# Experts' tokens by indirect DMA, and seven experts' results as DRAM rows, in a two-layer trunk on one core

## The chip, the core and the metric

The program runs on one NeuronCore of one Trainium2 chip. Its five engines run their own instruction streams in order and wait for each other through semaphores: TensorE (PE, matrix products and transposes into PSUM), VectorE (DVE), ScalarE (ACT), GpSimd (POOL) and SyncE (SP, which here only issues DMAs). ACT, POOL and SP can issue DMAs. The metric is the device time of one execution in microseconds (us); the number to be forecast is the median over several runs.

## The reference, cut to what matters

The model is a trunk of two layers over 256 latent tokens of width 1024. The second layer ends in a mixture of experts: each token picks two of eight experts, and each expert is a SwiGLU whose three matrices have 1024 x 3584 elements, all float32.

```
def moe_swiglu(h, w_router, b_router, w_gate, w_up, w_down):
    logits = (h @ w_router + b_router).astype(jnp.float32)
    top_v, top_i = lax.top_k(logits, TOP_K)              # TOP_K = 2
    weights = jax.nn.softmax(top_v, axis=-1)
    combine = jnp.sum(jax.nn.one_hot(top_i, N_EXPERTS) * weights[..., None], axis=-2)
    y = jnp.zeros_like(h)
    for e in range(N_EXPERTS):                           # 8
        y = y + combine[..., e:e + 1] * swiglu(h, w_gate[e], w_up[e], w_down[e])
    return y
...
    h_lat = modulate(rms_norm(x, norm_g[layer, 1]), sh_f, sc_f)
    x = x + g_f[:, None, :] * ffn(h_lat)
    return rms_norm(x, final_g)
```

## The kernel before

The change lies in the expert stage, the last 1000 us of the program. Everything else streams weights through the same machinery and stays as it is.

**Weights.** They come in units of 1 MB (128 x 2048 float32). SP loads each unit into one of 11 buffers of a ring (`load`, L162). To get float32 accuracy, a unit is split into a high part `wh` (ACT, L177) and a low part `wl` (DVE, L178), each in 3 rotating buffers, and each product is three matmuls of 512 columns (`mm3`, L214 to L216): high times high, low times high, high times low. One unit feeds 12 matmuls.

**Experts.** An expert holds up to 128 tokens and takes seven chunks of its hidden width. A chunk is six units: two of the gate and two of the up matrix (`expert_in`, the result is `a`), four transposes of `a` (`turn`, L1043), and two of the down matrix (`expert_out`), whose sums over the chunks stay in two PSUM tiles `ys` until the expert ends. That is 72 matmuls a chunk and 56 chunks. A branch at the end repeats an expert for tokens beyond 128; it isn't taken for these inputs.

**Getting the tokens.** The normalized residual lies as tokens x features in two SBUF tiles, `hth` (high part) and `htl` (low part). `pos` gives each token's place in each expert. `slots` makes the 256 x 128 one-hot matrix `S` of an expert on DVE (L961), and `gather` multiplies it with `hth` and `htl` for each of 8 blocks of 128 features (L996, 32 matmuls of 128 columns; the first two experts take 48, since the row scale is not yet in the tiles). ACT (L1000) and DVE (L1001) add the shift and make the high and low part of `xg`, the experts' input. Expert 0's gather runs at once, before anything else of the stage; the others run in the background of the expert before. `normalize` scales `hth` and `htl` in the background after that.

**Adding the results.** When experts 0 to 6 end, `scatter_steps` takes `ys` times the gate `gf` (DVE, L1070), splits it into `yh` and `yl`, multiplies with the transposed one-hot matrix `ST` (`slots_T`, L1063, two transposes; L1077, eight matmuls of 512 columns), and DVE adds the result with the token's weight to the accumulator `acc` (L1079). Expert 7 does the same without the split (`scatter_now`), since nothing is left to hide it. In expert 7's fourth chunk two loads fetch `fg`, the final norm's gain, into the buffers that `yh` and `yl` had:

```
fg = [mop.tile([P, 512], F32, tag=t, name=nm("fg"), bufs=1) for t in ("yh", "yl")]
for n in range(2):
    nc.scalar.dma_start(fg[n], A["fg_row"][:, 512 * n:512 * n + 512])
```

**Order.** The code is written in Tile: a scheduler sets each engine's order and the semaphores from the code's order and its own estimate of times, so background work is placed where it sees room. Tiles of one tag share their buffers, and whoever takes a buffer waits for its last reader.

Of the kernel before, what the change touches and what calls it, by code (L numbers as in the profile page):

```python
# [8 lines left out]
F32 = mybir.dt.float32  # L9
# [7 lines left out]
P = 128  # L17
KD = 8
# [94 lines left out]
def _program(tc, A, out):  # L113
# [10 lines left out]
    smallp = tc.alloc_tile_pool(name="smallp", bufs=2)  # L124
    xp = newpool("xp", 1, "right")
    pools = [const, rawp, whp, psp, smallp, xp]
# [119 lines left out]
    mc = const.tile([P, 392], F32, tag="mc", name="mc")  # L246
# [733 lines left out]
    def gather(p_, e, raw=False):  # L980
        S = []
        xg = mop1.tile([P, KD, 2, P], F32R, tag="xg", name=nm("xg"), bufs=2)

        def steps():
            if raw:
                s_ = slots(p_, e, "yh", rsh.bitcast(F32))
                terms = [(hth, s_), (htl, s_), (hth, slots(p_, e, "yl", rsl))]
            else:
                S.append(slots(p_, e))
                terms = [(hth, S[0]), (htl, S[0])]  # L990
            yield
            for k in range(KD):
                pg = ps_mm() if front and k % 2 else ps_t()
                for i_, (hsrc, s_) in enumerate(terms):
                    for tt in range(2):
                        pe.matmul(pg[:, 0:P], lhsT=hsrc[:, tt, k * P:k * P + P], rhs=s_[:, tt * P:tt * P + P],  # L996
                                  start=(i_ == 0 and tt == 0), stop=(i_ == len(terms) - 1 and tt == 1))
                b = mod[:, 1, 24 + k, 0:1]
                hi, lo = xg[:, k, 0, :], xg[:, k, 1, :]
                ia = act.activation(hi, pg[:, 0:P], AF.Identity, bias=b)  # L1000
                iv = vec.scalar_tensor_tensor(lo, pg[:, 0:P], b, hi.bitcast(F32), ALU.add, ALU.subtract)  # L1001
                hold[:] = [ia, iv] if front else []
                yield
            if raw:
                S.append(slots(p_, e))
        return xg, S, steps()

    front = []
# [76 lines left out]
    def scatter_steps(e, ys, ST):  # L1085
# [246 lines left out]
```

## Time and profile before

| what | value |
|---|---|
| runs | 1862.95, 1863.76, 1865.36 us (median 1863.76) |
| the profiled execution | 1863.94 us, its span 1862.1 us (1.84 us lie outside the span) |
| granted TensorE clock | full in every slice of the span |
| expert stage in that span | about 845 to 1846 us, then 16 us of last scatter, final norm and output |
| PE busy over the span | 1818.9 us, 98% |
| DVE, ACT busy over the span | 1331.7 us (72%), 1040.2 us (56%) |

Busy time is the time in which an engine had an instruction in work. PE's ends are modelled, so the distance from one matmul's start to the next one's is a better measure of its pace than the durations. All times of the trace are of the one profiled execution, counted from the span's start.

### The profile page before, as it was taken

How to read it: one execution, taken by the hardware profiler on the slowest of the kernel's cores; microseconds unless marked ns; L12 is line 12 of the kernel's file. 1: busy time of each engine (PE TensorE's matmuls, PEld its weight loads, DVE VectorE, ACT ScalarE, POOL GpSimd, SP SyncE). 2: the span in 40 equal slices, each digit the busy share in tenths (PEclk: the TensorE clock that was granted, in tenths of full speed). 3: DMA queues.
4: the chain of work that ended last, by engine and by line, in shares of the span. 5: the costliest groups of instructions: out<-in, count | busy, mean ns of one | idle time of the engine just before them, and what ended most of it. 6: DMA issues, size and time to landing. Idle time of an engine off the chain costs nothing. (4 is left out here: it accounts for less than half of the span.)

```text
span 1862.1 us, 22324 instructions
## 1 busy us (share of the span) xinstructions
PE 1818.9 (98%) x8878; PEld 1437.5 (77%) x8878; DVE 1331.7 (72%) x1452; ACT 1040.2 (56%) x1082; POOL 0.2 (0%) x4
## 2 busy tenths in 40 slices
PE   6999999999999999999999999999999999999997
PEld 4775487888888877488888888888888888888885
DVE  5632755443344586658899889898888898988987
ACT  3323634222222354646677777677777777777774
POOL 0000000000000000000000000000000000000000
PEclk9999999999999999999999999999999999999999
DMA  9567333232223254367999999999999999999890
GB/s 361 187 237 269 111 117 125 99 139 91 90 91 102 99 150 156 136 226 293 351 334 367 346 355 371 329 362 364 338 346 361 353 355 350 353 359 352 324 420 35
DMA packets 68688, 475.05 MB, mean 255 GB/s; under 512 B 7520, under 2 KB 8160, under 8 KB 13024
## 3 DMA queue, kind: packets, MB, share of 16 engines
q1 hardware_dynamic: 66416, 469.27, 68.0%
q10 hardware_dynamic: 2160, 4.27, 0.7%
q8 instruction: 72, 1.18, 0.2%
q14 instruction: 40, 0.33, 0.1%
HBM read 470.36 MB, written 1.05 MB: 253 GB/s over the span
## 5 line engine op out<-in xcount | busy, mean ns | idle before, releaser
L178 DVE TENSOR_TENSOR wl<-raw,wh 128x2048 fp32r<-128x2048 f32 (+1 forms) x461 | 904.9, 1984 | 242.4 <-ACT wh L177 238.1
L177 ACT ACTIVATE wh<-raw 128x2048 fp32r<-128x2048 f32 (+1 forms) x461 | 763.7, 1670 | 352.0 <-PE mm L215 133.6
L214 PE MATMUL mm<-wh,xg 128*128 128x512 f32 x896 | 353.4, 394 | 0.0
L215 PE MATMUL mm<-wl,xg 128*128 128x512 f32 x896 | 352.3, 393 | 0.0
L216 PE MATMUL mm<-wh,xg 128*128 128x512 f32 x896 | 349.9, 390 | 0.0
L215 PEld LDWEIGHTS mm<-wl,xg 128*128 128x128 f32 x896 | 168.4, 188 | 35.1 <-DVE wl L178 1.9
L216 PEld LDWEIGHTS mm<-wh,xg 128*128 128x128 f32 x896 | 168.4, 188 | 34.2
L214 PEld LDWEIGHTS mm<-wh,xg 128*128 128x128 f32 x896 | 168.4, 188 | 33.6
L214 PE MATMUL mm<-hx,wh 128*128 128x512 f32 (+1 forms) x496 | 189.0, 389 | 3.0 <-ACT hx L378 3.0
L215 PE MATMUL mm<-hx,wh 128*128 128x512 f32 (+1 forms) x496 | 191.4, 386 | 0.1
L216 PE MATMUL mm<-hx,wl 128*128 128x512 f32 (+1 forms) x496 | 191.0, 385 | 0.0
L215 PE MATMUL pss<-wl,ahi 128*128 128x512 f32 x448 | 176.7, 395 | 1.3 <-DVE wl L178 1.3
L216 PE MATMUL pss<-wh,alo 128*128 128x512 f32 x448 | 174.5, 390 | 0.0
L214 PE MATMUL pss<-wh,ahi 128*128 128x512 f32 x448 | 168.2, 391 | 0.0
L214 PEld LDWEIGHTS mm<-hx,wh 128*128 128x128 f32 x496 | 93.3, 189 | 26.3 <-ACT hx L378 3.4
L215 PEld LDWEIGHTS mm<-hx,wh 128*128 128x128 f32 x496 | 93.6, 189 | 18.7 <-DVE hx L380 0.5
L216 PEld LDWEIGHTS mm<-hx,wl 128*128 128x128 f32 x496 | 93.6, 189 | 18.7
L215 PEld LDWEIGHTS pss<-wl,ahi 128*128 128x128 f32 x448 | 84.2, 188 | 20.3 <-DVE wl L178 3.9
L214 PEld LDWEIGHTS pss<-wh,ahi 128*128 128x128 f32 x448 | 84.1, 188 | 17.2
L216 PEld LDWEIGHTS pss<-wh,alo 128*128 128x128 f32 x448 | 84.2, 188 | 16.7
L387 DVE SCALAR_TENSOR_TENSOR x<-mm,mod,x 128x256 f32<-128x256 f32 x120 | 52.4, 479 | 50.5 <-PE mm L216 50.5
L214 PE MATMUL mm<-ah,wh 128*128 128x512 f32 x176 | 68.6, 390 | 0.2
(275 smaller groups left out, 1975.7 us busy)
## 6 DMA issues: line engine op xcount, KB each, us to landing
raw<-in_mg SPq DMA_DIRECT2D x112, 1024.0 KB, 7.0
raw<-in_mu SPq DMA_DIRECT2D x112, 1024.0 KB, 7.1
raw<-in_md SPq DMA_DIRECT2D x112, 1024.0 KB, 6.9
raw<-in_ada SPq DMA_DIRECT2D x48, 1024.0 KB, 5.6
raw<-in_na_in SPq DMA_DIRECT2D x10, 1024.0 KB, 5.6
raw<-in_fg SPq DMA_DIRECT2D x10, 1024.0 KB, 4.9
raw<-in_fu SPq DMA_DIRECT2D x10, 1024.0 KB, 4.9
raw<-in_fd SPq DMA_DIRECT2D x10, 1024.0 KB, 4.9
```

What stands on the lines that cost most here:

```text
L177: act.activation(h_, r_, AF.Copy)
L178: vec.tensor_tensor(l_, r_, h_.bitcast(F32), ALU.subtract)
L214: pe.matmul(ps, lhsT=lh, rhs=rh, start=start, stop=False)
L215: pe.matmul(ps, lhsT=lh, rhs=rl, start=False, stop=False)
L216: pe.matmul(ps, lhsT=ll, rhs=rh, start=False, stop=stop)
L387: vec.scalar_tensor_tensor(x[:, db, a:b], ps[:, a:b], mod[:, l, g0 + db, c:c + 1], x[:, db, a:b], ALU.mult, ALU.add)
```

## The change

Two DRAM tiles are added: `hrow`, the 256 normalized tokens as rows of 1024 float32, and `yrow`, 7 x 128 rows for the results of experts 0 to 6. `normalize` now starts at once in the background: eight transposes and two ACT copies make the shift as rows, eight DVE operations make the complete token rows, and four POOL DMAs write them to `hrow`. Expert 0 is gathered as before (`first_gather_steps`). For experts 1 to 7 two small matmuls turn `S` into the list of token numbers, DVE converts it to integers, POOL issues one indirect DMA that fetches 128 rows (512 KB) into `xt`, and eight transposes in two groups with two splits make `xg`. When experts 0 to 6 end, ACT copies the two PSUM tiles `ys` to SBUF and issues two DMAs to `yrow` (`keep_rows`). `row_numbers` works out, for each token, its up to two rows in `yrow` and their weights; `combine`, in the background of expert 7, fetches them by four indirect DMAs of 512 KB and adds them to `acc`. Expert 7's own tokens are still added by `scatter_now`. Lines after the first hunk shift (L178 is L181 after, L1001 is L1005, L1043 is L1067, L1144 is L1213).

```diff
+    hrow = dramp.tile([TL, 1024], F32, tag="hrow", name="hrow")
+    yrow = dramp.tile([(NE - 1) * P, 1024], F32, tag="yrow", name="yrow")
...
     def normalize():
+        shift = []
+        for n in range(2):
+            pt = ps_t()
+            for j in range(4):
+                pe.transpose(pt[:, j * P:j * P + P], mod[:, 1, 24 + 4 * n + j, 0:1].to_broadcast([P, P]), ident)
+            shift.append(mop.tile([P, 512], F32, tag=("yh", "yl")[n], name=nm("shift"), bufs=1))
+            act.activation(shift[n], pt, AF.Copy)
+            yield
         for tt in range(2):
             for n in range(2):
...
-                    vec.tensor_scalar(t, l.bitcast(F32), r, None, ALU.mult)
+                    vec.scalar_tensor_tensor(t, l.bitcast(F32), r, shift[n], ALU.mult, ALU.add)
                 vec.scalar_tensor_tensor(t, h.bitcast(F32), r, t, ALU.mult, ALU.add)
+                nc.gpsimd.dma_start(hrow[tt * P:tt * P + P, 512 * n:512 * n + 512], t)
                 yield
-                put_split(h, l, t)
...
+    def gather(p_, e):
+        xg, S = new_xg(), []
+        def steps():
+            S.append(slots(p_, e))
+            yield
+            pi = ps_t()
+            for tt in range(2):
+                pe.matmul(pi[:, 0:2], lhsT=S[0][:, tt * P:tt * P + P].bitcast(F32), rhs=tokn[:, tt, :],
+                          start=(tt == 0), stop=(tt == 1))
+            idx = mop1.tile([P, 1], I32, tag="idx", name=nm("idx"), bufs=2)
+            vec.tensor_copy(idx, pi[:, 0:1])
+            xt = mop1.tile([P, 1024], F32, tag="htl", name=nm("xt"))
+            nc.gpsimd.indirect_dma_start(xt[:, :], None, hrow[:, :], bass.IndirectOffsetOnAxis(ap=idx[:, 0:1], axis=0))
+            for _ in range(4):
+                yield
+            for h in range(2):
+                pg = ps_t()
+                for j in range(4):
+                    pe.transpose(pg[:, j * P:j * P + P], xt[:, (4 * h + j) * P:(4 * h + j) * P + P], ident)
+                hi, lo = xg[:, 4 * h:4 * h + 4, 0, :], xg[:, 4 * h:4 * h + 4, 1, :]
+                put_split(hi, lo, pg.rearrange("p (k s) -> p k s", s=P))
+                yield
...
+    def keep_rows(e, ys):
+        for n in range(2):
+            yv = mop.tile([P, 512], F32, tag=("yh", "yl")[n], name=nm("yv"), bufs=1)
+            act.activation(yv, ys[n], AF.Copy)
+            nc.scalar.dma_start(yrow[e * P:e * P + P, 512 * n:512 * n + 512], yv)
+    def row_numbers():
...
+    def combine():
+        for tt in range(2):
+            yy = mop1.tile([P, 2, 1024], F32, tag="hth", name=nm("yy"))
...
+            for i_ in range(2):
+                vec.tensor_copy(ri[i_], rows[i_][0][:, tt:tt + 1])
+                nc.gpsimd.indirect_dma_start(yy[:, i_, :], None, yrow[:, :],
+                                             bass.IndirectOffsetOnAxis(ap=ri[i_][:, 0:1], axis=0))
+            for _ in range(3):
+                yield
+            for n in range(2):
+                h_ = slice(512 * n, 512 * n + 512)
+                a, b = yy[:, 0, h_], yy[:, 1, h_]
+                vec.tensor_scalar(a, a, rows[0][1][:, tt:tt + 1], None, ALU.mult)
+                vec.scalar_tensor_tensor(a, b, rows[1][1][:, tt:tt + 1], a, ALU.mult, ALU.add)
+                yield
+                vec.tensor_tensor(a, a, gf[:, h_], ALU.mult)
+                vec.tensor_tensor(acc[:, tt, h_], acc[:, tt, h_], a, ALU.add)
+                yield
...
     def finish():
         expert_out(prev["e"], prev["c"], prev, prev["ys"])
         if prev["c"] == NCH - 1:
-            pend[:] = [scatter_steps(prev["e"], prev["ys"], prev["ST"])]
-            next(pend[0])
+            keep_rows(prev["e"], prev["ys"])
...
-                ST = slots_T(S[0])
                 if e < NE - 1:
-                    nxt = gather(pos, e + 1, e == 0)
+                    nxt = gather(pos, e + 1)
                     background.append(nxt[2])
-                if e == 0:
-                    background.append(normalize())
+                else:
+                    ST = slots_T(S[0])
+                    background.append(combine())
+                if e == 1:
+                    background.append(row_numbers())
```

The scheduler decides where these pieces land, so three places of its order are shown.

On PE, while expert 2 runs, its order before holds the first of expert 3's eight gather groups between two chunks (`S_8744` is expert 3's one-hot matrix, `xg_7775` expert 2's input):

```order
L216 MATMUL pss_8552<-wh_8666,alo_8634 128x512
L1063 MATMUL pst_8719<-c_ident,S_7795 128x128 x2
L214 MATMUL mm_8725<-wh_8685,xg_7775 128x512
...
L216 MATMUL mm_8725<-wh_8703,xg_7775 128x512
L996 MATMUL pst_8765<-S_8744,hth 128x128 x2
L996 MATMUL pst_8765<-S_8744,htl 128x128 x2
L1043 MATMUL pst_8774<-c_ident,a_8626 128x128 x4
L214 MATMUL mm_8783<-wh_8728,xg_7775 128x512
```

After, PE makes the list of token numbers (L1016) and, one chunk of 72 matmuls later, transposes the first half of the fetched rows (L1027); a second chunk later, the second half:

```order
L217 MATMUL mm_8496<-wh_8462,xg_7699 128x512
L1016 MATMUL pst_8659<-tokn,S_8638 128x2 x2
L218 MATMUL mm_8496<-wl_8463,xg_7699 128x512
...
L217 MATMUL mm_8619<-wh_8584,xg_7699 128x512
L1027 MATMUL pst_8788<-c_ident,xt_8664 128x128 x4
L218 MATMUL mm_8619<-wl_8585,xg_7699 128x512
...
L217 MATMUL mm_8751<-wh_8717,xg_7699 128x512
L1027 MATMUL pst_8825<-c_ident,xt_8664 128x128 x4
```

The 32 gather matmuls and the two transposes L1063 are gone from the stretch; the index matmuls and the first transposes stand 72 matmuls apart, and that distance is the same for experts 3 to 7 (167 for expert 1, 72 for expert 2).

On DVE, at the first gather, the order before goes from the one-hot matrix `S` straight to the eight low parts of `xg` (six of the rows stand here):

```order
L961 TENSOR_SCALAR S_6438<-mc,pos_6340 128x128 x2
L1001 SCALAR_TENSOR_TENSOR xg_6359<-pst_6366,mod,xg_6359 128x128
L1001 SCALAR_TENSOR_TENSOR xg_6359<-mm_6375,mod,xg_6359 128x128
L1001 SCALAR_TENSOR_TENSOR xg_6359<-pst_6384,mod,xg_6359 128x128
L1001 SCALAR_TENSOR_TENSOR xg_6359<-mm_6393,mod,xg_6359 128x128
L1001 SCALAR_TENSOR_TENSOR xg_6359<-pst_6402,mod,xg_6359 128x128
```

After, the small operations of `row_numbers` stand there:

```order
L964 TENSOR_SCALAR S_6832<-mc,pos_6344 128x128 x2
L1119 TENSOR_SCALAR nw_7988<-pos_6344 128x16
...
L1128 TENSOR_REDUCE nr_8014<-nv_7987 128x2
L1005 SCALAR_TENSOR_TENSOR xg_6363<-pst_6370,mod,xg_6363 128x128
L1129 TENSOR_TENSOR ne_7989<-nv_7987,nr_8014 128x16
...
L1128 TENSOR_REDUCE nr_8057<-nv_7987 128x2
L1005 SCALAR_TENSOR_TENSOR xg_6363<-mm_6379,mod,xg_6363 128x128
L1129 TENSOR_TENSOR ne_7989<-nv_7987,nr_8057 128x16
...
L1151 COPY nj_13286<-ni_8065 128x1
L1005 SCALAR_TENSOR_TENSOR xg_6363<-pst_6388,mod,xg_6363 128x128
```

Seven of them moved ahead of the first low part, eleven between the first and the second, seven between the second and the third.

In expert 7, the order of ACT before has the two loads of `fg` (L1144) in a row of splits:

```order
L1033 ACTIVATE a_13371<-mm_13334 128x512
L1065 ACTIVATE ST_13467<-pst_13464 128x256
L1144 DMA fg_13591<-in_fg_row 128x512
L177 ACTIVATE wh_13393<-raw_13277 128x2048
L1144 DMA fg_13592<-in_fg_row 128x512
L177 ACTIVATE wh_13411<-raw_13298 128x2048
```

After, ACT issues them among `keep_rows` of expert 6 (L1112, L1113), whose buffers they take:

```order
L1112 ACTIVATE yv_12801<-pss_12006 128x512
L1113 DMA yrow<-yv_12801 128x512
L180 ACTIVATE wh_12785<-raw_12680 128x2048
L1112 ACTIVATE yv_12804<-pss_12007 128x512
L1213 DMA fg_13189<-in_fg_row 128x512
L1113 DMA yrow<-yv_12804 128x512
L180 ACTIVATE wh_12810<-raw_12698 128x2048
L1213 DMA fg_13190<-in_fg_row 128x512
L180 ACTIVATE wh_12828<-raw_12728 128x2048
```

A little later DVE reaches `combine` (L1159 to L1163), between the splits `wl`; the second pair of rows (`yy_13284`) has the buffer of the first (`yy_13077`):

```order
L181 TENSOR_TENSOR wl_12829<-raw_12728,wh_12828 128x2048
L1159 TENSOR_SCALAR yy_13077<-yy_13077,nc_8019 128x512
L181 TENSOR_TENSOR wl_12859<-raw_12746,wh_12858 128x2048
L1160 SCALAR_TENSOR_TENSOR yy_13077<-yy_13077,nc_8062 128x512
...
L1163 TENSOR_TENSOR acc<-acc,yy_13077 128x512
L181 TENSOR_TENSOR wl_12983<-raw_12874,wh_12982 128x2048
L1061 TENSOR_TENSOR a_12968<-a_12968,mm_12979 128x512
L181 TENSOR_TENSOR wl_13001<-raw_12895,wh_13000 128x2048
L1159 TENSOR_SCALAR yy_13284<-yy_13284,nc_8019 128x512 x2
```

So `fg` moved from the fourth chunk of expert 7 ahead to where the results of expert 6 are put away, and all of `combine` stands within 12 splits of the first.

## Rows read from the trace of the kernel before

**Rows 1.** Page, part 1: busy time, share of the span, instructions.
```profile
PE 1818.9 (98%) x8878; PEld 1437.5 (77%) x8878; DVE 1331.7 (72%) x1452; ACT 1040.2 (56%) x1082; POOL 0.2 (0%) x4
```

**Rows 2.** Windows: stretch and length; PE, PEld, DVE, ACT, POOL busy; clock, DMA share, GB/s.
```profile
845.00:1846.00 1001.00, 995.17 (x4625) 822.45 (x4625) 886.55 (x607) 725.40 (x538) 0.00 (x0) 1.00 0.91 344
1200.00:1300.00 100.00, 98.94 (x457) 81.76 (x456) 90.59 (x60) 73.26 (x53) 0.00 (x0) 1.00 0.95 362
1780.50:1797.00 16.50, 16.50 (x76) 13.65 (x76) 14.63 (x9) 12.09 (x9) 0.00 (x0) 1.00 1.02 420
```

**Rows 3.** Waits of PE, 845 to 1846 us: total, times, longest.
```profile
PE pst L1043 <- DVE xg L1001: 2.8, 4, 0.7
PE pst L996 <- DVE xg L1001: 1.8, 5, 0.6
PE pss L215 <- DVE wl L178: 1.3, 4, 0.7
```

**Rows 4.** Timeline of PE at a wait: start, duration, engine, line, operation, count.
```profile
1173.93 0.45 PE L214 MATMUL mm<-wh,xg 128*128 128x512 f32 x1
1175.12 0.66 PE L1043 MATMUL pst<-c_ident,a 128*128 128x128 f32 x4 [0.74 <-DVE xg L1001]
```

**Rows 5.** Timeline of PE at a gather group and a `turn`.
```profile
1029.28 0.39 PE L216 MATMUL mm<-wh,xg 128*128 128x512 f32 x1
1029.51 0.33 PE L996 MATMUL pst<-S,hth 128*128 128x128 f32 x2
1029.67 0.39 PE L996 MATMUL pst<-S,htl 128*128 128x128 f32 x2
1029.90 0.62 PE L1043 MATMUL pst<-c_ident,a 128*128 128x128 f32 x4
1030.28 0.47 PE L214 MATMUL mm<-wh,xg 128*128 128x512 f32 x1
```

**Rows 6.** Timeline of PE at two of the router's small float32 products.
```profile
844.43 0.37 PE L937 MATMUL pss<-msk,ones 128*128 128x8 f32 x2
844.65 0.37 PE L946 MATMUL pss<-msk,ones 128*128 128x8 f32 x2
```

**Rows 7.** Groups of DVE by shape, 845 to 1862 us: busy, mean ns, idle before.
```profile
L178 DVE TENSOR_TENSOR wl<-raw,wh 128x2048 fp32r<-128x2048 f32 x333 | 757.0, 2290 | 85.8 <-ACT wh L177 81.9 <-DMA raw<-in_md 2.1 <-DMA raw<-in_mg 0.9
L1070 DVE TENSOR_TENSOR yv<-pss,gf 128x512 f32<-128x512 f32 x14 | 9.6, 688 | 0.1
L973 DVE SCALAR_TENSOR_TENSOR t<-hth,rs_y,t 128x512 f32<-128x512 f32 x4 | 3.0, 752 | 0.1
L972 DVE TENSOR_SCALAR t<-htl,rs_y 128x512 f32<-128x512 f32 x4 | 1.9, 486 | 0.0
```

**Rows 8.** Timeline of DVE: two small operations in sequence, two of the first gather.
```profile
839.00 0.16 DVE L318 TENSOR_TENSOR rs_t<-rs_t,rs_v 128x2 f32<-128x2 f32 x1
839.19 0.16 DVE L319 SCALAR_TENSOR_TENSOR rs_y<-rs_t,rs_y 128x2 f32<-128x2 f32 x1
...
847.79 0.35 DVE L1001 SCALAR_TENSOR_TENSOR xg<-pst,mod,xg 128x128 fp32r<-128x128 f32 x1 [0.85 <-ACT xg L1000]
848.46 0.35 DVE L1001 SCALAR_TENSOR_TENSOR xg<-mm,mod,xg 128x128 fp32r<-128x128 f32 x1 [0.32 <-ACT xg L1000]
```

**Rows 9.** Timeline of PE: first record of the first gather's seventh group.
```profile
850.54 0.39 PE L996 MATMUL pst<-yh,hth 128*128 128x128 f32 x2
```

**Rows 10.** DMA issues: tiles, issuing queue, count, KB each, median us to landing.
```profile
raw<-in_md SPq DMA_DIRECT2D x112, 1024.0 KB, 6.9
...
out<-fo ACTq DMA_DIRECT2D x2, 256.0 KB, 3.1
```

**Rows 11.** Timeline of DVE: three splits back to back.
```profile
1750.19 6.70 DVE L178 TENSOR_TENSOR wl<-raw,wh 128x2048 fp32r<-128x2048 f32 x3
```

**Rows 12.** Waits of SP's DMA queue, 1000 to 1800 us.
```profile
SPq L162 <- DVE wl L178: 531.0, 213, 4.7
```

**Rows 13.** Timeline of SP: the last loads of the program.
```profile
1804.32 7.98 SPq L162 DMA_DIRECT2D raw<-in_md  x4
```

More of the change, by code (lines that the diff above doesn't have):

```diff
@@ L971, in normalize @@
                 with tc.issue_after(first_gather[1].ins):
-                    vec.tensor_scalar(t, l.bitcast(F32), r, None, ALU.mult)
+                    vec.scalar_tensor_tensor(t, l.bitcast(F32), r, shift[n], ALU.mult, ALU.add)
                 vec.scalar_tensor_tensor(t, h.bitcast(F32), r, t, ALU.mult, ALU.add)
+                nc.gpsimd.dma_start(hrow[tt * P:tt * P + P, 512 * n:512 * n + 512], t)
                 yield
-                put_split(h, l, t)
-                yield
[L980 to L1002, printed above, removed]
@@ new lines, in new_xg, with first_gather_steps @@
+    def new_xg():
+        return mop1.tile([P, KD, 2, P], F32R, tag="xg", name=nm("xg"), bufs=2)
+    def first_gather_steps(xg):
+        s_ = slots(pos, 0, "yh", rsh.bitcast(F32))
+        terms = [(hth, s_), (htl, s_), (hth, slots(pos, 0, "yl", rsl))]
+        for k in range(KD):
+            pg = ps_mm() if k % 2 else ps_t()
+            for i_, (hsrc, s_) in enumerate(terms):
+                for tt in range(2):
+                    pe.matmul(pg[:, 0:P], lhsT=hsrc[:, tt, k * P:k * P + P], rhs=s_[:, tt * P:tt * P + P],
+                              start=(i_ == 0 and tt == 0), stop=(i_ == len(terms) - 1 and tt == 1))
+            b = mod[:, 1, 24 + k, 0:1]
+            hi, lo = xg[:, k, 0, :], xg[:, k, 1, :]
+            ia = act.activation(hi, pg[:, 0:P], AF.Identity, bias=b)
+            iv = vec.scalar_tensor_tensor(lo, pg[:, 0:P], b, hi.bitcast(F32), ALU.add, ALU.subtract)
+            hold[:] = [ia, iv]
@@ new lines, in _program @@
+    rows = []
+    def combine():
+        for tt in range(2):
+            yy = mop1.tile([P, 2, 1024], F32, tag="hth", name=nm("yy"))
+            ri = [mop1.tile([P, 1], I32, tag=f"nj{i_}", name=nm("nj"), bufs=2) for i_ in range(2)]
+            for i_ in range(2):
+                vec.tensor_copy(ri[i_], rows[i_][0][:, tt:tt + 1])
[12 more added lines that the diff above has]
+                yield
@@ L1096, in _program @@
     prev = None
-    xg, S, g = gather(pos, 0, True)
-    front.append(0)
-    drain(g)
-    front.clear()
+    xg = new_xg()
+    first_gather_steps(xg)
     first_gather = list(hold)
@@ L1115, in _program @@
     vec.tensor_tensor(cw, cw, ws.unsqueeze(2).to_broadcast([P, 2, 8]), ALU.mult)
-    nxt, pend = (xg, S, g), []
+    nxt = (xg, [], iter(()))
+    tokn = mop1.tile([P, 2, 2], F32, tag="tokn", name="tokn")
+    vec.tensor_copy(tokn, mc[:, 392:396].rearrange("p (t c) -> p t c", c=2))
+    base = mc[:, 396:404]
+    background.append(normalize())
     def between():
@@ L1120, in between @@
             turn(prev)
-        if pend:
-            next(pend[0], None)
     def finish():
```

45 lines of the change are left out of this document (31 added, 14 removed).

## Prediction

> **What bounds the kernel now.** I read the table of engines first: GpSimd does nothing before [rows 1]. Then windows over the expert stage: PE is busy 995 of 1001 us at full clock, DVE 887, ACT 725, and the DMA engines move 344 GB/s [rows 2]. The reader is to see that PE sets the time and that whatever leaves its queue shortens the stage, while DVE has little room (89%). PE's waits then say how much of its queue is idle: 13 waits, 5.9 us in all, nine of them for the gather's low parts on DVE, four for a split [rows 3]. The timeline shows that such a wait costs more than its idle time: start to start one took 1.19 us where a matmul takes 0.23, so 0.96 is lost while 0.74 shows as idle [rows 4], 0.22 more. Last, SP: its loads wait 531 of 800 us for DVE to free a raw buffer [rows 12], so the loads are paced by the engines.
>
> **The change, part by part.** All sums are against the profiled execution, 1863.94 us; the median of the runs is 0.2 below it.
>
> *Removed from PE.* A 512-column matmul takes 0.23 us start to start (1029.28 to 1029.51), the four gather matmuls 0.39 and so 0.1 each [rows 5]. Experts 1 to 7 lose 240 gather matmuls (six times 32 and one 48): 240 x 0.1 = 24.0. Experts 0 to 6 lose eight 512-column scatter matmuls each: 56 x 0.227 = 12.7. Seven `slots_T` are 14 transposes; four transposes took 0.38 us and made the next matmul 0.08 longer [rows 5], 0.115 each: 1.6. Together 38.3.
>
> *Added to PE.* 56 transposes of fetched rows and 8 of the shift, 64 x 0.115 = 7.4. The index matmuls (14, two columns wide, float32) have no row; the router's products of 8 columns start 0.22 us apart and last 0.37 [rows 6], a 128-column one takes 0.1: 14 times 0.1 to 0.37 is 1.4 to 5.2, and I take 0.22, the nearest rows' spacing: 3.1. Net: -38.3 + 10.5 = -27.8.
>
> *Stalls removed.* The 13 waits of PE go with the gathers and scatters that cause them: 5.9 + 13 x 0.22 = -8.8. If the four waits for a split stay, 6.6.
>
> *DVE and ACT.* An expert's background costs DVE less than before (no eight low parts, no `yv`, `yl`, four accumulations; instead two splits of 512 columns). Neither engine gains time for the kernel, since PE waits for neither in between. I cost this at nothing; the cover is DVE's 11% of room.
>
> *First gather.* The 25 operations of `row_numbers` now stand between the first three low parts of `xg`. Small dependent operations start 0.20 us apart; the low parts came 0.67 apart, the first at 847.79 [rows 8]. Seven operations (1.4) behind `S`, which ended at about 846.94 (847.79 less the 0.85 idle), put the first low part at 848.3; it takes 0.35, eleven more 2.2, the second 0.35, seven more 1.4, so the third starts at 852.6 and ends at 853.0. PE's seventh group needs its PSUM buffer; it had begun at 850.54 [rows 9]. The experts' matmuls come behind it: +2.4 (0 to 4).
>
> *Writing the normalized rows.* Eight DVE operations of 0.75 [rows 7] and four DMAs from one buffer `t`: the second, third and fourth pair on DVE wait until the write before has landed. A 256 KB write landed in 3.1 us with nothing beside it, a 1 MB load beside others in 6.9 [rows 10]; I take 5. DVE stands with its splits behind each of three waits; three splits ahead [rows 11] hide most: +3 (0 to 8). The first fetch waits for all four writes, but its first transposes stand 167 matmuls behind, 38 us.
>
> *Fetching.* From the index matmuls to the first transposes lie 72 matmuls, 16.4 us. In it must pass: the conversion on DVE (behind up to three splits, 6.7 us [rows 11]), the issue on POOL and 512 KB (3.1 to 6.9 [rows 10]). That is 10 to 14 us and an issue without a row. I take it as hidden but for PSUM buffers and shorter waits at experts 1 and 2: +2 (0 to 8).
>
> *The end.* ACT's two loads of `fg` now take the buffers of expert 6's `yv`, so each waits in ACT's queue for a write to land, and the splits `wh` stand behind it: 1 to 5 us twice. DVE then waits for the gathers, which wait for the second write. `combine` itself is 4 x 0.49 + 4 x 0.75 + 8 x 0.69 = 10.4 us on DVE [rows 7], with 12 splits (27.5) and 2.7 of the chunk's own work among them, and the second pair of gathers, waiting for the first pair's buffer, has only 5 us of cover where it needs 3.1 to 6.9 twice: 41 us of work and about 6 of waits. PE has 12 x 12 x 0.227 + transposes = 33.6 us of work there. DVE is 13 behind, and two splits of lead (up to 5.5) are partly used up by ACT's own waits: +11 (3 to 22). This is the largest cost.
>
> *DMA.* 1 MB into `hrow`, 3.7 fetched, 3.7 into `yrow`, 2.1 fetched: 10.5 MB beside 344 [rows 2].
>
> **Sum.** -27.8 - 8.8 + 2.4 + 3 + 2 + 11 = -18.2: 1863.9 - 18.2 = 1845.7, and 0.2 less for the median: **1845.5**.
>
> **A rule weighed.** The price of a GpSimd DMA has no row here [rows 1]. The Trainium skill, page "SBUF — State Buffer", section "The 'DVE blocks DMA' trap" and "Who interferes with whom", states that descriptors of a DMA issued by GpSimd are written by GpSimd itself, which is locked out while DVE holds their shared ports, and that a DVE operation with two SBUF inputs contends with GpSimd's reads; it gives 620 ns alone and 3100 ns beside a DVE copy. By that an issue would wait for one split at least, which the 16.4 us of cover take, or for several, which is the second rival; no run here shows it yet.
>
> **Rivals.**
> 1. *The end is hidden* (0.13). If writes land in 3 us under load as they do alone [rows 10], and the lead of two splits is whole, the 11 and the 2 fall away: 1832. Against it: DVE's 41 us against PE's 34 is arithmetic of rows.
> 2. *The fetch is late* (0.16), the case on the other side. Place: POOL, between the conversion and the transposes of experts 1 to 7. If the issue too is held behind a run of splits (6.7), conversion, issue and landing make 6.7 + 6.7 + 6.9 = 20.3 against 16.4 us of cover: 4 us late, seven times, 28 on top: 1873.5. It decides from 18.2 / 7 = 2.6 us late. For it: DVE is 89% busy and three splits do run together [rows 11]. Against: a run of three occurs only after a wait for a chunk's end, and it would have to come twice in one chunk.
> 3. *DMA becomes the bound* (0.08). The last loads are issued by 1812 [rows 13], so 344 MB took 967 us. With 10.5 more in 18.2 us less it needs 355 / 949 = 374 GB/s. At 362, what a whole 100 us stretch showed [rows 2], loads would take 980 us, and the kernel 13 more than before: 1877. Below 367 GB/s the change loses. Against it: 420 GB/s over 16.5 us [rows 2], and loads that wait for buffers [rows 12]. The Trainium skill, page "DMA: Bandwidth & Descriptors", section "Specifications", gives about 358 GB/s for a core's share of the HBM, which would make it 24 us more than before, 1888; the stretch at 420 disagrees.
> 4. *The end is twice as dear* (0.10). If writes and gathers land in 7 us or more, ACT waits 10 and DVE 12: 22 instead of 11, 1856.
>
> **How the numbers follow.** My forecast, 1845.5 with its own range 1837 to 1855 (its terms' ends, not all at once), has 0.53. This kernel's runs differ by 0.13%, so I call no change what lies within 0.2%, 1860 to 1867.5. Faster: forecast, rivals 1 and 4 and a fetch that is late by under 2 us: 0.53 + 0.13 + 0.10 + 0.01 = 0.77. Same: fetches 2 to 3 us late and the DMA's edge, 0.07. Slower: the rest of rivals 2 and 3, 0.16. The range: below 1831 I leave a part of rival 1 (0.04), above 1866 the slower cases (0.16): 1831 to 1866.
>
> **What would show it.** Right: the waits of PE for `xg` on DVE gone from experts 1 to 7; PE's matmul count in the stage lower by 240 + 56 + 14 - 64 - 14 = 232 before records are doubled; on ACT in expert 7 two DMA issues that wait for a landing; on DVE an idle time before L1159 that a gather ends, and behind it PE waiting for `wl`, about 11 us. Wrong: a wait of PE's transposes L1027 for the fetch (rival 2), splits that wait for raw loads (rival 3), or no wait in expert 7 (rival 1). A first gather more than 4 us longer would show that the small operations are dearer than taken.

## The result, and the profile after

The changed kernel takes 1879.97 us (median of 4 runs, 1877.88 to 1883.31) against 1864.32 for the kernel before: a ratio of 1.0086, with a 95% interval from 1.0073 to 1.0098. It is slower by 16 us, where 18 us of gain were forecast. The profiled execution took 1879.57 us with a span of 1877.6. All medians here and below are of executions at full speed: one of `c_noplace` (3014 us) and one of the kernel before beside it (6448 us) ran in a much slower state and are left out.

The windows of the changed kernel over the same stretch as [rows 2], and over two slices in the last expert (stretch and length; PE, PEld, DVE, ACT, POOL busy; clock, DMA share, GB/s):

```profile
845.00:1846.00 1001.00, 975.31 (x4419) 794.83 (x4418) 851.15 (x570) 711.98 (x494) 20.23 (x15) 0.99 0.91 355
1740.00:1750.00 10.00, 5.99 (x13) 3.98 (x13) 2.72 (x3) 6.61 (x5) 1.09 (x2) 0.66 1.01 407
1780.00:1790.00 10.00, 4.80 (x11) 3.80 (x12) 7.81 (x7) 0.08 (x1) 0.00 (x0) 0.66 0.52 179
```

PE is idle for 26 us of this stretch where it was idle for 6, and in two slices the granted clock is 0.66 of full on average, where it had been 1.00 over the stage. PE's waits, which answer to [rows 3]:

```profile
PE mm L218 <- DVE wl L181: 16.9, 9, 6.8
PE pss L218 <- DVE wl L181: 5.2, 2, 3.7
PE mm L217 <- ACT wh L180: 3.5, 1, 3.5
```

All nine waits for the gather's low parts are gone. In their place stand 12 waits for splits of weights (lines L180 and L181, L177 and L178 before), 25.6 us, three of them long. No wait of the transposes of fetched rows (L1027) is among them, and none for a raw load.

A table by expert shows where the rest is. It gives the start of each expert's first unit matmul in the two traces, and in that of `c_all`, an experiment told below, and the distance to the next start (for expert 7, to the start of its last one):

```
expert     before: start, length   after: start, length   c_all: start, length
0            851.9   119.7           862.0   117.5           853.2   118.5
1            971.6   124.9           979.6   120.4           971.7   119.0
2           1096.5   124.8          1100.0   122.5          1090.7   120.3
3           1221.3   124.8          1222.5   122.0          1210.9   119.7
4           1346.1   125.3          1344.4   122.3          1330.6   119.7
5           1471.4   124.4          1466.7   121.9          1450.2   119.7
6           1595.7   124.4          1588.7   121.7          1569.9   119.4
7           1720.2   125.7          1710.4   150.1          1689.3   128.5
```

Experts 0 to 6 became 19.9 us shorter. But expert 0 starts 10.1 us late, expert 7 is 24.4 longer, and 0.9 is lost behind it: 10.1 - 19.9 + 24.4 + 0.9 = 15.5, the whole difference of the spans. The 10 us of the start are the strangest, since nothing ahead of the expert stage was changed but the width of one constant tile.

### The profile page after: what moved, and what is told of

It reads as the page before. It is cut to its first block, busy times and chain, and to the rows that moved or that the text cites. A ratio compares the mean times of both kernels' runs of the same rounds, so it can differ in the third digit from the quotient of the medians.

```text
span 1877.6 us, 21836 instructions
## 1 busy us (share of the span) xinstructions
PE 1813.6 (97%) x8660; PEld 1411.8 (75%) x8660; DVE 1300.4 (69%) x1393; ACT 1028.4 (55%) x1031; POOL 20.4 (1%) x19
## 5 line engine op out<-in xcount | busy, mean ns | idle before, releaser
L181 DVE TENSOR_TENSOR wl<-raw,wh 128x2048 fp32r<-128x2048 f32 (+1 forms) x461 | 901.8, 1983 | 256.7 <-ACT wh L180 249.0
L180 ACT ACTIVATE wh<-raw 128x2048 fp32r<-128x2048 f32 (+1 forms) x461 | 761.9, 1669 | 343.2 <-PE mm L218 135.8
L218 PE MATMUL mm<-hx,wh 128*128 128x512 f32 (+1 forms) x496 | 193.9, 391 | 0.1
L217 PE MATMUL mm<-hx,wh 128*128 128x512 f32 (+1 forms) x496 | 191.0, 393 | 3.0 <-ACT hx L381 3.0
L218 PE MATMUL pss<-wl,ahi 128*128 128x512 f32 x448 | 181.8, 406 | 5.2 <-DVE wl L181 5.2
L217 PE MATMUL pss<-wh,ahi 128*128 128x512 f32 x448 | 163.4, 396 | 0.0
L219 PEld LDWEIGHTS pss<-wh,alo 128*128 128x128 f32 x448 | 84.7, 189 | 18.2
L222 ACT ACTIVATE ahi<-pst 128x512 fp32r<-128x512 f32 x56 | 33.5, 599 | 75.8 <-PE pst L1067 75.8
```

Source lines behind the costliest of these rows:

```text
L180: act.activation(h_, r_, AF.Copy)
L181: vec.tensor_tensor(l_, r_, h_.bitcast(F32), ALU.subtract)
L217: pe.matmul(ps, lhsT=lh, rhs=rh, start=start, stop=False)
L218: pe.matmul(ps, lhsT=lh, rhs=rl, start=False, stop=False)
L219: pe.matmul(ps, lhsT=ll, rhs=rh, start=False, stop=stop)
L222: return (act.activation(hi, src, AF.Copy), vec.tensor_tensor(lo, src, hi.bitcast(F32), ALU.subtract))
```

## The experiments

The times are medians; the ratio is to the kernel before on the same chip, with its 95% interval.

**1. Four kernels on the 10 us ahead of the expert stage.** In the trace no wait was longer there; PE's matmuls stood farther apart. The diff widens the constant tile `mc` from 392 to 404 columns, and that moves every tile allocated after it by 64 bytes, while the tiles on the other side of SBUF stay.

```diff
# b_mc404 (the kernel before)
-    mc = const.tile([P, 392], F32, tag="mc", name="mc")
+    mc = const.tile([P, 404], F32, tag="mc", name="mc")
# b_mc404_gap: b_mc404, and
-    wp.tile([P, 32], F32, tag="gap", name="gap", bufs=1)
+    wp.tile([P, 48], F32, tag="gap", name="gap", bufs=1)
# a_mc424 (the changed kernel)
-    mc = const.tile([P, 404], F32, tag="mc", name="mc")
+    mc = const.tile([P, 424], F32, tag="mc", name="mc")
# a_align: a_mc424, and
-    mop.tile([P, 56], F32, tag="gap", name="gap2", bufs=1)
+    mop.tile([P, 48], F32, tag="gap", name="gap2", bufs=1)
```

> The kernel before, with nothing changed but the constant tile mc, 404 instead of 392 columns wide (the 12 columns are never read). It moves every SBUF tile allocated after it by 64 bytes, the weight buffers wh and wl among them, and leaves the tiles on the other side, hx among them, where they were. Theory 1, the 10 us that the changed kernel lost before the expert stage come from where the two operands of a matmul lie to each other: about 10 us slower than before, 1874, and the loss grows over the first 700 us. Rival, the loss comes with the change itself (DRAM tiles, another program to fetch): 1864, no change.

> As b_mc404, and an unused gap on the other side is 64 bytes wider, so that hx moves by the same 64 bytes as wh and wl. Theory 1 in the form that the distance of the two operands matters: back to 1864. In the form that the place of wh and wl alone matters: stays at 1874. Rival (the change itself): 1864, as b_mc404.

> The changed kernel with mc 424 columns wide (20 of them unused), so that wh and wl lie 128 bytes from where the kernel before had them, and the distance to hx is the old one again modulo 128. Theory 1: 10 us faster than the changed kernel, about 1870, all of it before the expert stage; the down projections of the expert stage stay slow (0.233 us a matmul instead of 0.227), since ahi and alo moved by another amount. Rival: 1880, no change.

> As a_mc424, and the unused gap ahead of ahi and alo is 32 bytes narrower, so that their distance to wh and wl is that of the kernel before modulo 128. Theory 1: the 10 us and another 7 (1344 down matmuls, 0.006 us each, and some neighbours): about 1863. Rival: 1880, no change.

Measured: `b_mc404` 1873.5 (1.0046, 1.0030 to 1.0063), `b_mc404_gap` 1874.2 (1.0049, 1.0032 to 1.0065), `a_mc424` 1881.3 (1.0085, 1.0068 to 1.0102), `a_align` 1877.8 (1.0069, 1.0053 to 1.0086). So twelve columns that nobody reads cost the kernel before 9 us, which settles that the loss does not come with the DRAM tiles or the fetches. But my modulus, 128 bytes, was wrong: the three kernels that should have got the time back (`b_mc404_gap`, `a_mc424`, `a_align`) did not.

Each matmul of the traces was then set beside the places of its operands in the built program. The mean distance from start to start, and the distance in bytes between the operands' places modulo 256:

```
kernel        hx and wh   us      ahi and wh   us      xg and wh   us
before             0    0.2270          0    0.2272          0    0.2280
b_mc404          192    0.2333          0    0.2273          0    0.2280
b_mc404_gap      128    0.2328          0    0.2272          0    0.2281
after            192    0.2333        160    0.2324          0    0.2282
a_mc424          128    0.2329        160    0.2333          0    0.2283
a_align          128    0.2329        128    0.2323          0    0.2277
```

`wh` moved by 64 bytes in three of these kernels and by 128 in two, and the third column, whose tiles all move along, keeps its pace: the distance counts, not the place. The table has `hx` as the moving operand (512 columns) and `wh` as the stationary one. With the roles turned, 288 products ahead of the stage, the same two tiles show a smaller loss in two of these kernels: 0.228 us in the kernel before, 0.229 in `b_mc404` and the changed kernel, 0.232 to 0.233 in the three others. So it also counts which of the two moves.

**2. The modulus of 256 bytes.** Two more kernels make all these distances multiples of 256.

```diff
# b_mc456 (the kernel before)
+    mc = const.tile([P, 456], F32, tag="mc", name="mc")
# a_al256 (the changed kernel)
+    mc = const.tile([P, 456], F32, tag="mc", name="mc")
+    mop.tile([P, 16], F32, tag="gap", name="gap2", bufs=1)
```

> The kernel before, with the constant tile mc 456 columns wide (64 of them never read), so that wh and wl move by 256 bytes against hx. In the traces so far a 512-column matmul takes 0.227 us where the places of its two operands differ by a multiple of 256 bytes and 0.233 where they don't (hx against wh: 0.227 in the kernel before, 0.233 with mc at 404 and in both kernels with a shift of 128 bytes). Theory 1, a multiple of 256 bytes is what counts: 1864.5, no change against the kernel before. Rival, any wider mc (its load, its tensor in DRAM) costs the time: 1874, as with 404 columns.

> The changed kernel with mc 456 columns wide and the unused gap ahead of ahi and alo 160 bytes narrower, so that hx, xg, ahi and alo all lie a multiple of 256 bytes from wh and wl. Theory 1: 10 us less before the expert stage and about 7 less in its down projections: 1863. Rival (the place does not count): 1880.

Measured: `b_mc456` 1864.2 (1.0002, 0.9992 to 1.0012), `a_al256` 1862.0 (0.9993, 0.9982 to 1.0004). Theory 1 holds with this modulus: a wider tile than that of 404 columns costs nothing when the step is 256 bytes, and the changed kernel wins back 18 us. PE's timeline shows it in a chain of 192 matmuls of `hx` with `wh` and `wl` that no wait interrupts, first and last of it, in `b_mc404`:

```profile
480.87 0.39 PE L214 MATMUL mm<-hx,wh 128*128 128x512 f32 x1
...
525.57 0.40 PE L216 MATMUL mm<-hx,wl 128*128 128x512 f32 x1
```

and in `b_mc456`:

```profile
475.30 0.39 PE L214 MATMUL mm<-hx,wh 128*128 128x512 f32 x1
...
518.86 0.39 PE L216 MATMUL mm<-hx,wl 128*128 128x512 f32 x1
```

The same 192 matmuls take 44.70 and 43.56 us. The durations shown beside them (0.39 and 0.40) tell nothing, since ends are modelled; only starts show it. In `a_al256` the first matmul of expert 0 starts at 852.18 where the changed kernel's starts at 862.03, and experts 0 to 6 take 841.4 us in place of 848.4: 10 us of the 18 lie ahead of the stage and 7 in experts 0 to 6, for the most part in their down projections. The start scatters: in the six profiled kernels that lay out `mc`, `hx` and `wh` as the changed kernel does, expert 0 begins between 858.0 and 863.5, so a difference of 2 or 3 us there is not read.

**3. The last expert.** What the trace of the changed kernel shows there, first ACT's timeline:

```profile
1728.99 0.36 ACTq L1213 DMA_DIRECT2D fg<-in_fg_row  x1
1729.20 0.58 ACT L1112 ACTIVATE yv<-pss 128x512 f32<-128x512 f32 x1
1729.81 0.33 ACTq L1113 DMA_DIRECT2D yrow<-yv  x1
1730.24 1.91 ACT L180 ACTIVATE wh<-raw 128x2048 fp32r<-128x2048 f32 x1 [0.46 <-ACT yv L1112]
1738.33 0.36 ACTq L1213 DMA_DIRECT2D fg<-in_fg_row  x1
1738.81 1.91 ACT L180 ACTIVATE wh<-raw 128x2048 fp32r<-128x2048 f32 x1 [6.66 <-DMA raw<-in_mu]
```

The second load of `fg` is issued 8.5 us after the write of `yrow` whose buffer it takes, and the split behind it waits 6.66 us (the first load hardly waited); the name in the bracket is that of a raw load which had its share in that wait, but the issue at 1738.33 stands ahead of it in the queue. POOL's gathers:

```profile
1739.22 0.94 POOL L1152 DMA_INDIRECT yy<-yrow,nj  x1 [111.03 <-DMA yrow<-yv]
1740.46 0.94 POOL L1152 DMA_INDIRECT yy<-yrow,nj  x1 [0.30 <-issue]
1770.10 2.75 POOL L1152 DMA_INDIRECT yy<-yrow,nj  x1 [28.70 <-DVE acc L1163]
1773.15 2.69 POOL L1152 DMA_INDIRECT yy<-yrow,nj  x1 [0.30 <-issue]
```

and DVE, which waits for them with its splits behind it:

```profile
1749.57 0.49 DVE L1159 TENSOR_SCALAR yy<-yy,nc 128x512 f32<-128x512 f32 x1 [6.53 <-DMA yy<-yrow,nj]
...
1778.44 0.88 DVE L1159 TENSOR_SCALAR yy<-yy,nc 128x512 f32<-128x512 f32 x2 [3.41 <-DMA yy<-yrow,nj]
1782.19 0.75 DVE L1160 SCALAR_TENSOR_TENSOR yy<-yy,nc 128x512 f32<-128x512 f32 x1 [2.87 <-DMA yy<-yrow,nj]
```

A gather takes about 10 us from issue to its rows, and the second pair is asked for only when DVE has let go of the first pair's buffer. Two kernels take these apart.

```diff
# a_fg_pool (the changed kernel)
-                    nc.scalar.dma_start(fg[n], A["fg_row"][:, 512 * n:512 * n + 512])
+                    nc.gpsimd.dma_start(fg[n], A["fg_row"][:, 512 * n:512 * n + 512])
# a_late (the changed kernel): all four gathers at once, into hth and htl
+        for tt in range(2):
+            yy.append(mop1.tile([P, 2, 1024], F32, tag=("hth", "htl")[tt], name=nm("yy")))
+            for i_ in range(2):
...
+        for _ in range(6):
+            yield
...
+                with tc.issue_after(last_a[0].ins):
+                    vec.tensor_scalar(a, a, rows[0][1][:, tt:tt + 1], None, ALU.mult)
```

(`last_a` holds the last chunk's `a * up` product on DVE.)

> The changed kernel with the two loads of fg issued by POOL instead of ACT, so that ACT's splits no longer stand behind a load that waits for a write of expert 6's rows to land. Theory 2, the two waits in expert 7 add up (ACT's 6.6 us at 1738, then DVE's 6.5 at 1749): the first loss of PE, about 6 us and 2 more at the lower clock, goes: 1872. Rival, the gathered rows land at 1749.5 whatever ACT does, and DVE waits for them in order ahead of the next split: PE's stall only moves, 1878 to 1880.

> The changed kernel with both pairs of rows gathered at once into two buffers (hth and htl) and combine's DVE operations spread over expert 7's chunks 4 to 6, behind each chunk's own product. The loads of fg stay on ACT. Theory 2, PE lost its time to DVE's waits for gathers that were not there yet: the losses at 1748 (4.1 and 2 at the lower clock) and at 1778 (7.0 and 3) go, those at 1737 stay: about 1864. Rival, DVE has too much work there (12 splits, 27 us, and 10.4 of combine against PE's 33) and the wait is only where it shows: at most 5 us faster, 1875.

Measured: `a_fg_pool` 1879.2 (1.0085, 1.0068 to 1.0102), `a_late` 1867.0 (1.0017, 1.0007 to 1.0028). In `a_fg_pool` theory 2 fell and the rival held: ACT's wait is gone and PE has one long wait instead of three, as its waits say:

```profile
PE pss L218 <- DVE wl L181: 19.1, 3, 14.4
```

The gathered rows set the time, whatever ACT did before. `a_late` won 13 us, nearer to theory 2's 16 than to the rival's 5; its expert 7 takes 138.6 us instead of 150.1. It asks for the rows earlier and also uses them later, and no run separates the two. The longest wait that is left in expert 7 is ACT's (of the 12.4 us on `wl`, 7.8 are the six expert ends of the next experiment):

```profile
PE mm L218 <- DVE wl L181: 12.4, 13, 1.5
PE mm L217 <- ACT wh L180: 3.6, 1, 3.6
```

**4. The end of each expert.** At six expert ends PE lost 1.4 us (1.7 at one). ACT's timeline at one:

```profile
1360.41 0.60 ACT L1112 ACTIVATE yv<-pss 128x512 f32<-128x512 f32 x1 [0.56 <-PE pss L219]
1361.04 0.33 ACTq L1113 DMA_DIRECT2D yrow<-yv  x1
1361.74 1.92 ACT L180 ACTIVATE wh<-raw 128x2048 fp32r<-128x2048 f32 x1 [0.74 <-DVE alo L223]
1363.57 0.58 ACT L1112 ACTIVATE yv<-pss 128x512 f32<-128x512 f32 x1
```

and what DVE and then PE did with it:

```profile
1363.69 2.29 DVE L181 TENSOR_TENSOR wl<-raw,wh 128x2048 fp32r<-128x2048 f32 x1 [2.46 <-ACT wh L180]
...
1366.04 0.50 PE L218 MATMUL mm<-wl,xg 128*128 128x512 f32 x1 [1.54 <-DVE wl L181]
```

The split `wh` stands behind a copy that waits for the expert's last matmul, and behind its DMA.

```diff
# a_keep_pool (the changed kernel)
-            nc.scalar.dma_start(yrow[e * P:e * P + P, 512 * n:512 * n + 512], yv)
+            nc.gpsimd.dma_start(yrow[e * P:e * P + P, 512 * n:512 * n + 512], yv)
# a_keep_dve: a_keep_pool, and
-            act.activation(yv, ys[n], AF.Copy)
+            vec.tensor_copy(yv, ys[n])
```

> The changed kernel with keep_rows' two DMAs issued by POOL, its copies still on ACT. Theory 3: the issues are 0.7 of the 1.9 us that ACT spends, so half of the 1.4 us at each end goes: 1876. Rival (the wait for the expert's last matmul, not the work, makes ACT late): 1879 to 1880.

> The changed kernel with keep_rows' two copies made by DVE instead of ACT, and its two DMAs issued by POOL. In the changed kernel PE loses 1.4 us at the end of each of six experts to a split wl that stands behind a split wh that stands behind keep_rows on ACT, while DVE is idle for 2.5 us. Theory 3, ACT's copies and issues (two of 0.6, two of 0.35, and the waits for the expert's last matmul) make the split late: 1.0 to 1.4 us less at each of six ends, 6 to 8 in all: 1873. Rival, the split is late because raw loads or the fetched rows are: 1880; or DVE's copies hold the splits just as ACT's did: 1878 to 1880.

Measured: `a_keep_pool` 1869.3 (1.0023, 1.0011 to 1.0036), `a_keep_dve` 1862.9 (0.9987, 0.9977 to 0.9996). Theory 3 holds at the ends: the loss of 1.41 us becomes 0.84 without the issues, and nothing without the copies, and experts 2 to 6 shorten by 1.2 to 1.6 us each. PE's waits over the whole stage in `a_keep_dve`, none of them at an expert's end:

```profile
PE pss L218 <- DVE wl L181: 6.7, 3, 2.8
PE mm L218 <- DVE wl L181: 2.8, 3, 1.8
```

Both gained more than expected, because expert 7 shortened too, from 150.1 to 143.9 and 139.0: I had not thought of it that expert 6's rows leave earlier once they do not go through ACT's queue. The changed kernel issued the second write at 1729.8 and the first gather at 1739.2, 9.4 us later; in `a_keep_dve` 5.7 us lie between them:

```profile
1720.21 0.54 POOL L1113 DMA_DIRECT2D yrow<-yv  x1 [0.46 <-DVE yv L1112]
1725.94 0.99 POOL L1152 DMA_INDIRECT yy<-yrow,nj  x1 [5.18 <-DMA yrow<-yv]
```

ACT still waits for a landing behind its loads of `fg` there, 4.6 us, but the gathered rows come earlier.

**5. The fetch half by itself.** Kernel `c_gather` has the fetches of the changed kernel and the scatter matmuls of the kernel before (no `yrow`, no `keep_rows`, no `combine`), with places a multiple of 256 bytes apart. In its trace, 23 matmuls of 512 columns stand between the index matmuls and the transposes for experts 4 to 7 (35 for expert 3), where the changed kernel has 72. `c_gather_far` waits three background steps more, and has 95 there (83 for expert 3).

```diff
# c_gather_far, on c_gather
-            for _ in range(4):
+            for _ in range(7):
                 yield
             for h in range(2):
                 pg = ps_t()
```

> One half of the change by itself: tokens fetched from DRAM rows as in the changed kernel, results scattered by matmuls as in the kernel before (no yrow, no keep_rows, no combine), with all operands a multiple of 256 bytes apart. Theory: the fetch half gives 240 x 0.1 us less of gather matmuls, 10.5 more of transposes and index products, 6 less of waits for the gather's low parts, 2 to 3 more for the writes of the rows: 1864.5 - 18 = 1847. Rival (the fetch is held up beside DVE's splits and takes back what it gives): 1864.

> As c_gather, with three more background steps between the index matmuls and the transposes of the fetched rows, which puts 98 matmuls (22 us) between them instead of 24 (5.5 us). Theory, in c_gather the fetch was late by 3.8 to 6.3 us five times (24 us) only because the transposes stood too near: the waits of L1027 go and the fetch half by itself gives about 17 us: 1848 to 1850. Rival, the fetch is held up by DVE however early it is asked for: still 1870 or more.

Measured: `c_gather` 1879.4 (1.0070, 1.0053 to 1.0087), `c_gather_far` 1844.4 (0.9898, 0.9881 to 0.9916). The first missed its expectation, and its waits show why:

```profile
PE pst L1027 <- DMA xt<-hrow,idx: 23.6, 5, 6.2
```

This is the rival of the late fetch, made real by a shorter distance. Behind each of these five waits PE ran at the lower clock level for a while: 31 of its 512-column matmuls took 0.426 us, 6 us more. With the distance restored the waits of L1027 are gone, and the fetch half alone makes the kernel 19 us faster; PE's waits in `c_gather_far` are

```profile
PE pss L218 <- DVE wl L181: 2.4, 7, 1.3
PE mm L218 <- DVE wl L181: 1.3, 1, 1.3
```

**6. The repairs together.** `c_all` is the changed kernel with the edits of `a_al256`, `a_late`, `a_fg_pool` and `a_keep_dve`. `c_noplace` is the same without those of `a_al256`. `c_best` is `c_all` with two more edits:

```diff
# c_best, on c_all
-                t, r = mop.tile([P, 512], F32, tag="yv", name=nm("t"), bufs=1), rs[:, tt:tt + 1]
+                t, r = mop.tile([P, 512], F32, tag="yv", name=nm("t"), bufs=2), rs[:, tt:tt + 1]
-            vec.tensor_copy(yv, ys[n])
+            vec.tensor_tensor(yv, ys[n], gf[:, 512 * n:512 * n + 512], ALU.mult)
...
+                o_ = acc[:, tt, h_]
+                    vec.scalar_tensor_tensor(o_, a, rows[0][1][:, tt:tt + 1], o_, ALU.mult, ALU.add)
+                vec.scalar_tensor_tensor(o_, b, rows[1][1][:, tt:tt + 1], o_, ALU.mult, ALU.add)
```

> The changed kernel with the four repairs together: places a multiple of 256 bytes apart (mc of 456 columns, the gap ahead of ahi 160 bytes narrower), combine late and with two buffers, fg loaded by POOL, keep_rows on DVE and POOL. Theory, the four losses are separate and add up: 1880 - 18 (places) - 13 (combine) - 8 (fg, which only counts once combine no longer hides it) - 7 (keep_rows) = 1834. Rival, they cover each other or DMA becomes the bound once PE waits less: 1848 (places and combine alone).

> c_all without the repair of places (mc of 404 columns, the gap as in the changed kernel). If places cost the same whatever else is repaired: 1836 + 18 = 1854. If part of the 18 us is hidden behind the other waits or the other way round: 1842 to 1850.

> c_all, with the gate gf multiplied in by keep_rows' copy (so that combine is eight DVE operations of 0.75 us, 6.0, instead of 10.4), and two buffers for the rows that are written to hrow. Theory, of PE's remaining waits in c_all about 3.8 us stand at combine and 4.1 at the row writes: 4 to 6 us less than c_all, 1831. Rival, those waits are DVE's splits whatever combine does: 1835 to 1836.

Measured: `c_all` 1836.0 (0.9845, 0.9820 to 0.9870), `c_noplace` 1849.4 (0.9933, 0.9911 to 0.9955), `c_best` 1830.9 (0.9825, 0.9808 to 0.9843). The four losses add up to within 2 us of what was expected of `c_all`. Places are worth 13 us here by the medians and 16 by the ratios (the two kernels ran on different chips), 18 in the changed kernel, which fits the second of `c_noplace`'s two expectations better than the first. In `c_best` PE's waits over the stage are

```profile
PE pss L218 <- DVE wl L181: 0.8, 1, 0.8
PE mm L218 <- DVE wl L181: 0.6, 2, 0.5
```

and it beats the kernel before by 1.75%.

## Why the prediction was wrong, point by point

**The sum for PE was right, within 3 us.** The net of removed and added matmuls (-27.8) and the stalls removed (-8.8), with +3 and +2 for the row writes and for experts 1 and 2, make -31.6. Of this 1.8 (expert 6's eight scatter matmuls) falls into expert 7's stretch, which leaves -29.8 for experts 0 to 6. `c_all`, in which the other losses are repaired, takes 836.1 us from the first start of expert 0 to that of expert 7 where the kernel before takes 868.3: -32.2. In `c_best`, which hardly waits for the row writes either, it is 833.1, or -35.2, and the sum without the +3 and +2 is -34.8. The waits for low parts went, as said, and PE has 218 records less over the span (8878 in [rows 1], 8660 after): the 232 of the prediction, with each of the 14 index matmuls recorded twice.

**The step that failed first is one that the sum does not have.** It prices operations and waits, and takes the 0.227 us of a matmul as given. The diff's twelve columns of `mc` (not among the lines of the diff shown ahead of the prediction), and the new layout of the expert stage's tiles, moved operands against each other: 1416 matmuls of `hx` ahead of the stage took 0.2333 us instead of 0.2270, and 1344 in its down projections 0.2324 instead of 0.2272. That is 8.9 of the 10 us at the start and 7.0 in the stage, and `b_mc404`, `b_mc456` and `a_al256` show it from both sides. (A part of the rest may be the clock. It was not full in every slice ahead of the stage: the granted clock was 0.50, its lower level, for 10.2 us of the kernel before, from 27.9 to 34.7 and from 287.3 to 290.7, and in the changed kernel for 3.4 us more, from 230.1 to 233.5, behind waits of PE of 1.0 and 2.0 us; that is 1.7 us at most.) The edit stood in the diff, and I gave it no line.

**"I cost this at nothing; the cover is DVE's 11% of room."** That step weighs DVE's load alone; `keep_rows` on ACT came under it at nothing without a reason of its own. It cost 1.4 us at each of six ends, 8.7 in all (start to start; `a_keep_dve` has none of it). The copy (0.60) and the issue (0.33) are short, but stand in ACT's order ahead of a split and behind a wait for the expert's last matmul. How much of the loss a copy on ACT behind the split would keep, no run shows.

**The end was the largest cost, and its size was too small.** I put +11 (3 to 22). Expert 7 became 24.4 us longer although expert 6's scatter (1.8) left it. Behind the sixth expert end, five waits of PE cost it 17.4 there (start to start, less the 0.227 of a matmul), and the clock 5 more: 22. The mechanisms were the named ones: a load of `fg` behind a landing (one of the two, not both), DVE behind gathers. Two durations were off. The DMAs of the changed kernel, which answer to [rows 10] (KB each where the view has them, median us to landing):

```profile
yrow<-yv ACTq DMA_DIRECT2D x14, 256.0 KB, 7.8
hrow<-t POOLq DMA_DIRECT2D x4, 256.0 KB, 4.5
...
xt<-hrow,idx POOLq DMA_INDIRECT x7, 9.2
yy<-yrow,nj POOLq DMA_INDIRECT x4, 9.6
```

A write beside the loads took 7.8, above my upper end of 6.9, and a gather 9.6. And I had no term for the clock: in the two slices shown, which hold PE's long waits, the granted clock is 0.66 on average, its lower level of 1.2 GHz for a part of each, and behind these waits about 26 matmuls of the expert took 0.427 us instead of 0.227, 5 us in all. Starts of two of them (0.43 apart; PE had just waited 3.46 and 1.82 us):

```profile
1744.12 0.63 PE L217 MATMUL mm<-wh,xg 128*128 128x512 f32 x1
1744.55 0.63 PE L218 MATMUL mm<-wl,xg 128*128 128x512 f32 x1
```

My fourth rival had the size of this, 22, though by waits alone.

**The first gather: +2.4 forecast, 0.1 measured.** From the first of six matmuls just ahead of the gather (L920) to the first expert matmul it took 6.90 us (855.13 to 862.03), against 6.78 before (845.10 to 851.88). DVE's first low parts and the small operations among them:

```profile
857.72 0.16 DVE L1128 TENSOR_REDUCE nr<-nv 128x2 f32<-128x16 f32 x1
857.82 0.35 DVE L1005 SCALAR_TENSOR_TENSOR xg<-pst,mod,xg 128x128 fp32r<-128x128 f32 x1
...
859.16 0.34 DVE L1005 SCALAR_TENSOR_TENSOR xg<-mm,mod,xg 128x128 fp32r<-128x128 f32 x1
```

Eleven operations and a low part took 1.34 us, not 2.5: only those that depend on the one just ahead start 0.20 to 0.25 apart, the others 0.07 to 0.13.

**The fetch was hidden, as forecast.** The conversion and 9.2 us from issue to landing fit into 16.4 us of cover; `c_gather` shows what happens with 5.2 (23 matmuls). **DMA was not the bound:** `c_best` moves 358 MB in the 990 us from 820 to 1810, PE waits for no raw load there, and DVE for ten, none over 0.9 us and 5.7 in all.

So the fourth rival was near in what it named, and none in its sum: the change loses by three things at once, of which the prediction had one, at half its price. Places 15.9, `keep_rows` 8.7 and the end 11 beyond its 11 make 36 us. The first gather (2.3) and the waits of the row writes and the fetch (1.7 measured, 5 forecast) came out cheaper, which leaves 30 of the 33.7 us between the forecast of -18.2 and the +15.5 of the spans; the other 3 are not assigned.

## What to carry to other kernels

A diff that changes the size of any tile changes the places of all tiles behind it: compare the pace of matmuls that it does not touch, start to start, and where it moved, look at the distance between the moving and the stationary operand (here a multiple of 256 bytes was 2.3 to 2.8% faster in the two groups of the table). An engine with room to spare still delays the critical one when an operation that waits stands ahead of one that is needed: price an added operation by what it waits for and by what is queued behind it. And a transfer that somebody waits for in order should be asked for as early as its data allow, into a buffer of its own; 95 matmuls of distance in place of 23 turned 14 us lost into 19 won.

## What the runs showed of the hardware

- The pace of a 512-column float32r matmul depends on where its two operands lie to each other: 0.227 to 0.228 us at a multiple of 256 bytes, 0.232 to 0.233 at 128, 160 and 192 bytes off (the six kernels of the table). Which of the two moves counts as well: `wh` moving against a stationary `hx` took 0.229 in `b_mc404`, where `hx` moving against `wh` took 0.233. Why, no run shows.
- The eleven indirect gathers of the changed kernel (128 rows of 4 KB each) took 8.2 to 12.9 us from issue to landing, 256 KB written to DRAM beside the weight loads 7.8 in the median of 14 to `yrow` and 4.5 of four to `hrow`, against 3.3 for a write at the program's end.
- Issuing an indirect DMA cost POOL 0.94 to 0.97 us in seven of the changed kernel's eleven cases, 2.7 to 3.0 in the others. It depends on whether a split has begun on DVE. POOL in the changed kernel:

```profile
1259.24 0.94 POOL L1021 DMA_INDIRECT xt<-hrow,idx  x1 [121.06 <-DVE idx L1019]
...
1625.43 2.76 POOL L1021 DMA_INDIRECT xt<-hrow,idx  x1 [121.01 <-DVE idx L1019]
```

and DVE beside them:

```profile
1259.28 4.49 DVE L181 TENSOR_TENSOR wl<-raw,wh 128x2048 fp32r<-128x2048 f32 x2
...
1625.08 4.49 DVE L181 TENSOR_TENSOR wl<-raw,wh 128x2048 fp32r<-128x2048 f32 x2
```

The first issue began 0.04 us before a split; the second 0.35 into one, and ended 0.82 after that split did (1625.08 + 2.29 = 1627.37). In `c_gather` an issue at 1269.20 beside a split from 1268.85 took 2.75 as well. In the 13 profiled kernels that have such issues, all 57 that began inside a split ended 0.81 to 0.88 us after it, and the 78 others took 0.93 to 1.00. An ordinary DMA issue of POOL is not held: 80 that began inside a split took 0.54 to 0.59 us, 50 others 0.54 to 0.74. One of them, 0.39 us into a split that had begun at 878.08:

```profile
878.47 0.58 POOL L985 DMA_DIRECT2D hrow<-t  x1 [6.62 <-DVE t L984]
```

The Trainium skill, page "SBUF — State Buffer", section "Who interferes with whom", says that a DVE instruction with two SBUF inputs, as a split is, contends with a GpSimd instruction that reads SBUF, and that the order of issue decides who blocks. This trace agrees where the split is first: the held issues are those that are given a list of row numbers, and the hold ended with the split, so it was one split long, never the several of the prediction's second rival. Where the issue is first the trace shows no block: the split that began 0.04 us behind the issue at 1259.24, and the one behind it, took 4.49 us together, as the pair at 1625.08 did.
